# One fused two-block forward pass on one core: where the VectorE work of 128 gathered tokens stands in its queue, and which engine writes a fourth of the one-hots

## The chip, the core and the metric

The kernel runs on one core of one Trainium2 chip. Its time is in device microseconds (us), the median of its runs. The profile names the engines PE (TensorE: matmul, and PEld for its weight loads), DVE (VectorE), ACT (ScalarE), POOL (GpSimd) and SP (SyncE, which only issues DMAs here); a trailing q is the engine's queue. [...]

## What is computed

The reference runs two blocks of two layers each on 256 tokens of 1024 channels. The first block is a mixer (an mLSTM, a block attention and a compressed attention side by side) and a feed-forward of 4096 channels. The second block works on the 256 tokens and, in its first layer, on 256 context tokens too: attention, and then a layer of experts picked by product keys:

```python
v1, i1 = lax.top_k(s1, 16)
v2, i2 = lax.top_k(s2, 16)
top_s, pos = lax.top_k(cand_s, 16)
expert = jnp.take_along_axis(cand_i, pos, axis=-1)
g = jax.nn.softmax(top_s, axis=-1)
act = jax.nn.gelu(jnp.einsum('nhkd,nd->nhk', u_tab[expert], hb))
w = g * act
out = jnp.einsum('nhk,nhkd->nd', w, v_tab[expert])
```

There are 16384 experts with one row of 1024 numbers in each table. A token has 8 heads with 16 experts each, so 128 chosen experts. All is in float32.

## The kernel before

**Split products.** A matmul in this kernel multiplies operands that are cut in two: `split` (line 207) has ACT round the operand to the matmul's format (line 209) and DVE subtract that from the operand (line 210). `mac` (lines 243 to 245) then issues three matmuls, high by high, high by low and low by high. Weights come through `load` (line 118) in tiles of 512 KB on SP's queue, and the two halves lie in the ring `ws`, four buffers, so two weight tiles at a time.

**The order of the work.** Instructions are traced in program order by Python generators. The tile framework then orders each engine's queue by its own plan: an instruction whose inputs the plan holds ready may go ahead of ones that were traced earlier. [...]

**The side generator.** Work on the context tokens is a generator, `aside` (line 1314): context attention, key scores, choice of experts, `spread` for one half of the context tokens, and last `gather` for the other half. The main program moves it on by so many steps at a time: `breathe` (line 92) and `beside` (line 98) in block one and in the second block's first attention, `ahead` (line 1129) by `GP[0]` steps for each expert tile, and the function `side` in `block2` (line 1346) by `GP[1]` steps for each expert tile. The rates stand at the top: `WM`, `WF` (block one), `FN` (line 38: four steps in the norm, and then so many for each yield of `qkv`, `attention` and `attn_out`) and `GP` (line 43).

**Dense experts and the spread.** For 384 rows (the 256 tokens and 128 of the context tokens) the expert layer is computed densely, 128 tiles of 128 experts. `ahead` runs `hidden` (line 1117) for each tile: load 512 KB of the u table, split it, 24 matmuls with 384 columns, gelu on ACT (line 1126), and store of 192 KB to `kept` in DRAM. This is the first hidden pass, about 1332 to 2062 us. `experts` (line 1146) then loads `kept` back, multiplies it by the gate weights G (line 1165), splits it and 512 KB of the v table, and sums in PSUM with 18 matmuls of 512 columns a tile. G comes in loads of 1536 KB for every 8 tiles. While it runs, `side` also moves `ada_rest` on by a step for each odd tile up to the 95th: a load of 512 KB (`in_ada_w`) and one or two DVE instructions (line 777). This is the first sum over experts, about 2062 to 2610 us. The second layer does the same for the 256 tokens (2837 to the end), with no side generator.

G is built by `spread` (line 1061): for every 4 tokens `ones` (line 1067) writes a stationary tile of four one-hots of 128 by 128 in f16, one instruction each on POOL (line 1071), and DVE writes the moving side with three instructions of 512 columns (line 1075). Eight matmuls of 128 columns follow (line 1089). All of it lies in one buffer of the ring `wb` (three buffers), which the loads of the tables also use later. `spread` runs five times with 32 batches: once for the context tokens (about 913 to 1023 us, beside the feed-forward of block one), twice in each hidden pass.

**The gathered tokens.** The other 128 context tokens are computed from their own 128 experts each, by `gather` (line 1275). A slot is the c-th expert of all 128 tokens. For each table there are 128 slots, so 256 in all. `fetch` (line 1282) issues two indirect DMAs on POOL (line 1286) for a pair of slots, 512 KB each, into one buffer of the ring `b8` (three buffers, one of which holds the activations and the sum). Of the first table each slot is a dot product on DVE (line 1304), of the second a weighted addition on DVE (line 1308, 1306 for the first). One step of the generator is one slot. A pair is fetched while the pair before it is computed.

Of the kernel before, what the change touches and what calls it, by code (L numbers as in the profile page):

```python
# [10 lines left out]
F32 = mybir.dt.float32  # L11
# [4 lines left out]
ALU = mybir.AluOpType  # L16
AX = mybir.AxisListType

P = 128
S = 256  # L20
D = 1024
# [13 lines left out]

WM = ({3: 1, 5: 2, 12: 3, 22: 1, 34: 1}, {12: 2, 14: 2, 18: 2, 22: 2, 26: 2, 32: 2, 34: 2, 37: 2})
WF = ((0, 2.0), (0, 3.5))
FN = (4, 2.0, 2.0, 2.0)

P0 = ((0, 1.0), (22, 1.0), (30, 0.8), (72, 0.8))  # L40
P1 = ((2, 1.0), (28, 0.8), (30, 0.72), (79, 0.8))

GP = (0.85, 0.6)

EAR = (1, 1)

# [11 lines left out]
class Net:  # L58
# [148 lines left out]
    def split(self, hi, lo, src):  # L207

        self.nc.scalar.copy(hi, src)  # L209
        self.nc.vector.tensor_sub(lo, src, hi.bitcast(F32))  # L210

    def cut_in_two(self, shape, raw):

# [847 lines left out]
    def spread(self, r, Gd, nb, pm="C", home="k8"):  # L1061


        nc = self.nc
        st, (r, r0) = None, r

        def ones(n):
            E = self.t("wb", [P, 4, 512], F16)
            first = E[:, 0].rearrange("p (j e) -> p j e", e=P)
            for j in range(4):  # L1070
                nc.gpsimd.tensor_scalar(first[:, j], self.iota16, r0[:, n + j:n + j + 1], None, ALU.is_equal)  # L1071
            pairs = [E[:, 1 + i].rearrange("p (h e j) -> p h e j", h=2, j=2) for i in range(3)]
            for i in range(3):
                col = r[:, i, n:n + 4].rearrange("p (h j) -> p h j", j=2)[:, :, None].to_broadcast([P, 2, P, 2])
                nc.vector.tensor_tensor(pairs[i], pairs[0] if i else self.iota2[:, None].to_broadcast([P, 2, P, 2]), col,
                                        op=ALU.mult if i else ALU.is_equal)
            return first, pairs

        E = ones(0)
        yield  # L1080
        for n in range(0, P, 4):
            q, m = divmod(n, NT)
            nxt = ones(n + 4) if n + 4 < P else None
            if m == 0:
                st = self.t(home, [P, P, NT])
            pG = self.p(pm, [P, 4, P])
            for j in range(4):
                for i in range(2):
                    nc.tensor.matmul(pG[:, j], E[0][:, j], E[1][1 + i][:, j // 2, :, j % 2], start=i == 0, stop=i == 1)  # L1089
            nc.scalar.activation(st[:, :, m:m + 4], pG.rearrange("p n e -> p e n"), AF.Copy, scale=1 / GSCALE)  # L1090
            if m == NT - 4:
                nc.sync.dma_start(Gd[:, nb + q], st)
            E = nxt
            yield
# [103 lines left out]
    @staticmethod  # L1198
    def col(mod, s, j):
        return mod[:, s, 8 * j:8 * j + 8]  # L1200
# [74 lines left out]
    def gather(self, idx, g, out):  # L1275


        nc, io = self.nc, self.io
        tables = io["u_rows"], io["v"][0].rearrange("a b d -> (a b) d")
        work = [(t, c) for t in tables for c in range(0, P, 2)]  # L1280

        def fetch(i):
            t, c = work[i]
            r = self.t("b8", [P, 2, D])
            for j in range(2):
                nc.gpsimd.indirect_dma_start(out=r[:, j], out_offset=None, in_=t,
                                             in_offset=bass.IndirectOffsetOnAxis(ap=idx[:, c + j:c + j + 1], axis=0))
            return r

        hr = self.t("b8", [P, 2, D])  # L1290
        nc.sync.dma_start(hr[:, 0], self.hrd)
        h, acc = hr[:, 0], hr[:, 1]
        act = self.t("act", [P, P], bufs=1)
        r = fetch(0)
        for i, (t, c) in enumerate(work):
            if i == P // 2:
                nc.scalar.activation(act, act, AF.Gelu_apprx_tanh)
                nc.vector.tensor_mul(act, act, g)
            nxt = fetch(i + 1) if i + 1 < len(work) else None
            for j in range(2):  # L1300
                a = act[:, c + j:c + j + 1]
                if i < P // 2:
                    junk = self.t("b2", [P, D], mybir.dt.bfloat16)
                    nc.vector.scalar_tensor_tensor(junk, r[:, j], 1.0, h, ALU.mult, ALU.mult, accum_out=a)
                elif i == P // 2 and j == 0:
                    nc.vector.tensor_scalar(acc, r[:, j], a, None, ALU.mult)
                else:
                    nc.vector.scalar_tensor_tensor(acc, r[:, j], a, acc, ALU.mult, ALU.add)  # L1308
                yield
            r = nxt  # L1310
        nc.sync.dma_start(out, acc)
        yield
# [14 lines left out]
    def block2(self, x):  # L1327
# [3 lines left out]

        hT = self.norm_T(fg, x, col(mod, 0, 1), col(mod, 0, 0), between=lambda: self.breathe(FN[0]))
        qT, kT, v = self.beside(self.qkv(fg, 0, hT, True), FN[1])
        oT = self.beside(self.attention(fg, qT, [(kTc, vc), (kT, v)]), FN[2])
        self.beside(self.attn_out(fg, 0, oT, col(mod, 0, 2), x), FN[3])
        hx = self.norm_T(fg, x, col(mod, 0, 4), col(mod, 0, 3), lambda k: (h[0][:, k, 0:S], h[1][:, k, 0:S]))
        hd = lambda k: (h[0][:, k], h[1][:, k])
        far = self.side
        plan = self.routing(0, [hx], Gd[0], ((0, 0), (1, 8)), EAR[0], P0)
        self.ahead(0, hd, ND, self.kept, 128, plan + [(0, far, GP[0], False), (100, self.ada_rest(MID, 48), 0.3, True)])  # L1340
        gates = self.t("k8", [P, 4, 512])
# [4 lines left out]
        def side(e):  # L1346
            if e % 2:
                next(rest, None)
            due[0] += GP[1]
            while due[0] >= 1:  # L1350
# [158 lines left out]
```

## Time and profile before

| | |
|---|---|
| median of 3 runs | 3632.98 us (3625.54 to 3647.02) |
| the profiled execution's own time | 3624.63 us |
| its span, first to last instruction | 3622.9 us |
| PE busy | 3248.7 us, 90% of the span |
| DVE busy | 2513.4 us, 69% |
| ACT busy | 1449.4 us, 40% |
| POOL busy | 978.2 us, 27% |
| moved by DMA | 803.17 MB, mean 222 GB/s |
| mean granted clock of TensorE | 0.953 |

A row of a stretch gives its start and end, its length, then the busy time of each engine with its number of instructions, then the granted clock, the mean busy share of the 16 DMA engines and the rate. A row of waits gives who waited for whom, with the total, the number of times and the longest one. Rows by source line give the number of instructions, their least, median and greatest duration in ns, and the start of the first and the last. A row of the timeline gives start, duration, engine and line, and in brackets the idle time before it with what ended that.

### The profile page before, as it was taken

The numbers are of one execution on the slowest core, as the hardware profiler recorded it, in microseconds if no ns is written. First come the engines' busy times: TensorE is split into PE (matmuls) and PEld (weight loads), VectorE is DVE, ScalarE is ACT, GpSimd is POOL, SyncE is SP. The second block draws the span as 40 slices with busy tenths as digits, with TensorE's granted clock in tenths as the row PEclk, the third lists the DMA queues.
The fourth block names the chain that finished last, engine by engine and source line by source line (L and its number), as shares of the span: only waits on it lengthen the run. The fifth ranks groups of instructions, "written<-read, shape, count | busy, mean of one in ns | idle before, by whom it ended". The sixth has DMA issues, their size and how long they took to land. (4 is left out here: it accounts for less than half of the span.)

```text
span 3622.9 us, 51227 instructions
## 1 busy us (share of the span) xinstructions
PE 3248.7 (90%) x18333; PEld 2772.2 (77%) x18333; DVE 2513.4 (69%) x5177; ACT 1449.4 (40%) x2465; POOL 978.2 (27%) x968
## 2 busy tenths in 40 slices
PE   8999899889756698887779899999989999999999
PEld 6676688768644597887779887777868999988777
DVE  6667556789667897887665576655577888656665
ACT  6543245633323342232223433333344555454443
POOL 0000000000954434787776000000010067830000
PEclk9999999979978899998889999999999999999999
DMA  7456454325467778887886788877523677688885
GB/s 241 151 180 204 151 164 146 108 89 172 159 223 245 253 267 300 291 290 266 287 274 228 254 283 276 266 251 251 178 66 101 198 243 264 241 281 291 288 258 188
DMA packets 340225, 803.17 MB, mean 222 GB/s; under 512 B 31105, under 2 KB 179585, under 8 KB 334593
## 3 DMA queue, kind: packets, MB, share of 16 engines
q1 hardware_dynamic: 303104, 665.66, 56.0%
q0 software_dynamic: 36864, 134.23, 10.8%
q8 instruction: 144, 2.36, 0.3%
q14 instruction: 113, 0.92, 0.1%
HBM read 713.00 MB, written 86.77 MB: 221 GB/s over the span
## 5 line engine op out<-in xcount | busy, mean ns | idle before, releaser
L209 ACT CAST ws<-w 128x1024 fp32r<-128x1024 f32 (+1 forms) x528 | 547.3, 1037 | 1048.8 <-PE psA L244 727.6
L210 DVE TENSOR_TENSOR ws<-w,ws 128x1024 fp32r<-128x1024 f32 (+1 forms) x528 | 640.7, 1215 | 255.3 <-ACT ws L209 253.5
L245 PE MATMUL psA<-b,ws 128*128 128x384 f32 (+1 forms) x2048 | 659.0, 322 | 105.2 <-DVE ws L210 104.3
L1071 POOL TENSOR_SCALAR wb<-iota,R 128x128 f16<-128x128 f16 x640 | 600.3, 954 | 382.3 <-ACT R L1054 279.1
L243 PE MATMUL psA<-b,ws 128*128 128x384 f32 (+1 forms) x2048 | 663.4, 324 | 3.6 <-ACT ws L209 3.6
L244 PE MATMUL psA<-b,ws 128*128 128x384 f32 (+1 forms) x2048 | 652.1, 318 | 0.0
L245 PEld LDWEIGHTS psA<-b,ws 128*128 128x128 f32 x2048 | 398.9, 195 | 119.9 <-DVE ws L210 118.7
L209 ACT CAST k<-wb 128x1024 fp32r<-128x1024 f32 x256 | 269.0, 1051 | 513.3 <-DMA wb<-in_v 513.2
L245 PE MATMUL psC<-k,k 128*128 128x512 f32 x1056 | 422.7, 400 | 25.9 <-DVE k L210 25.2
L243 PE MATMUL psC<-k,k 128*128 128x512 f32 x1056 | 418.6, 397 | 19.6 <-ACT k L209 19.6
L244 PE MATMUL psC<-k,k 128*128 128x512 f32 x1056 | 417.6, 396 | 3.6 <-DVE k L210 3.6
L243 PEld LDWEIGHTS psA<-b,ws 128*128 128x128 f32 x2048 | 399.8, 195 | 4.7 <-ACT ws L209 4.5
L244 PEld LDWEIGHTS psA<-b,ws 128*128 128x128 f32 x2048 | 398.4, 195 | 0.0
L210 DVE TENSOR_TENSOR k<-wb,k 128x1024 fp32r<-128x1024 f32 x256 | 312.4, 1220 | 81.9 <-ACT k L209 81.7
L158 POOL TENSOR_TENSOR rsrf<-rsvf,neghalf 128x1 f32<-128x1 f32 (+5 forms) x38 | 41.9, 1106 | 1206.6 <-DVE rsvf L157 1206.6
L244 PE MATMUL psC<-ws,k 128*128 128x512 f32 (+1 forms) x608 | 250.3, 412 | 25.5 <-DVE ws L210 25.4
L245 PEld LDWEIGHTS psC<-k,k 128*128 128x128 f32 x1056 | 199.2, 189 | 93.2 <-DVE k L210 49.4
L1165 DVE TENSOR_TENSOR k<-k,b 128x384 f32<-128x384 f32 (+1 forms) x256 | 123.7, 489 | 202.7 <-DMA k<-kept 197.8
L243 PE MATMUL psC<-ws,k 128*128 128x512 f32 (+1 forms) x608 | 246.9, 410 | 7.1 <-DVE k L197 4.5
L243 PEld LDWEIGHTS psC<-k,k 128*128 128x128 f32 x1056 | 199.5, 189 | 66.7 <-ACT k L209 23.8
L1308 DVE SCALAR_TENSOR_TENSOR b<-b,act,b 128x1024 f32<-128x1024 f32 x127 | 164.2, 1293 | 120.3 <-DMA b<-in_v,idx 119.7
L245 PE MATMUL psC<-ws,k 128*128 128x512 f32 (+1 forms) x608 | 246.1, 407 | 0.7 <-DVE k L716 0.6
(452 smaller groups left out, 6096.2 us busy)
## 6 DMA issues: line engine op xcount, KB each, us to landing
w<-in_u SPq DMA_DIRECT2D x256, 512.0 KB
wb<-in_v SPq DMA_DIRECT2D x256, 512.0 KB
w<-in_w_ff SPq DMA_DIRECT2D x128, 512.0 KB
wb<-in_ada_w SPq DMA_DIRECT2D x80, 512.0 KB
G<-k SPq DMA_DIRECT2D x32, 1024.0 KB
w<-in_wA SPq DMA_DIRECT2D x48, 512.0 KB
kept<-k SPq DMA_DIRECT2D x128, 192.0 KB
b<-G SPq DMA_DIRECT2D x16, 1536.0 KB
```

Source lines behind the costliest of these rows:

```text
L158: nc.gpsimd.tensor_tensor(r[:m, :cols], v[:m, :cols], self.neghalf[:m, :cols], op=ALU.pow)
L209: self.nc.scalar.copy(hi, src)
L210: self.nc.vector.tensor_sub(lo, src, hi.bitcast(F32))
L243: self.nc.tensor.matmul(out, ah, bh, start=first, stop=False)
L244: self.nc.tensor.matmul(out, ah, bl, start=False, stop=False)
L245: self.nc.tensor.matmul(out, al, bh, start=False, stop=last)
L1071: nc.gpsimd.tensor_scalar(first[:, j], self.iota16, r0[:, n + j:n + j + 1], None, ALU.is_equal)
L1165: nc.vector.tensor_mul(g3, g3, Gs[:, :, j])
L1308: nc.vector.scalar_tensor_tensor(acc, r[:, j], a, acc, ALU.mult, ALU.add)
```

## The change

`split` keeps its DVE subtraction in `self.mark`. Every DVE instruction of `gather` is traced inside `issue_after(self.mark)`: an edge without a semaphore that keeps it behind the subtraction traced last, in DVE's own queue. The rates `FN` and `GP` change. In `ones` the fourth of the four one-hots is written by DVE.

```diff
-FN = (4, 2.0, 2.0, 2.0)
+FN = (4, 1.5, 1.5, 1.5)
...
-GP = (0.85, 0.6)
+GP = (0.8, 0.9)
...
         self.nc.scalar.copy(hi, src)
-        self.nc.vector.tensor_sub(lo, src, hi.bitcast(F32))
+        self.mark = self.nc.vector.tensor_sub(lo, src, hi.bitcast(F32)).ins
...
             for j in range(4):
-                nc.gpsimd.tensor_scalar(first[:, j], self.iota16, r0[:, n + j:n + j + 1], None, ALU.is_equal)
+                eng = nc.vector if j == 3 else nc.gpsimd
+                eng.tensor_scalar(first[:, j], self.iota16, r0[:, n + j:n + j + 1], None, ALU.is_equal)
...
             for j in range(2):
                 a = act[:, c + j:c + j + 1]
-                if i < P // 2:
-                    junk = self.t("b2", [P, D], mybir.dt.bfloat16)
-                    nc.vector.scalar_tensor_tensor(junk, r[:, j], 1.0, h, ALU.mult, ALU.mult, accum_out=a)
-                elif i == P // 2 and j == 0:
-                    nc.vector.tensor_scalar(acc, r[:, j], a, None, ALU.mult)
-                else:
-                    nc.vector.scalar_tensor_tensor(acc, r[:, j], a, acc, ALU.mult, ALU.add)
+                with self.tc.issue_after(self.mark):
+                    if i < P // 2:
+                        junk = self.t("b2", [P, D], mybir.dt.bfloat16)
+                        nc.vector.scalar_tensor_tensor(junk, r[:, j], 1.0, h, ALU.mult, ALU.mult, accum_out=a)
+                    elif i == P // 2 and j == 0:
+                        nc.vector.tensor_scalar(acc, r[:, j], a, None, ALU.mult)
+                    else:
+                        nc.vector.scalar_tensor_tensor(acc, r[:, j], a, acc, ALU.mult, ALU.add)
                 yield
```

## Rows read from the trace of the kernel before

**Rows 1.** The page, part 1: busy us of each engine, share of the span, instructions.

```profile
PE 3248.7 (90%) x18333; PEld 2772.2 (77%) x18333; DVE 2513.4 (69%) x5177; ACT 1449.4 (40%) x2465; POOL 978.2 (27%) x968
```

**Rows 2.** Stretches from 1332 on: us, busy us of each engine, PEclk, DMA share, GB/s.

```profile
1332.00:1450.00 118.00, 100.78 (x519) 97.91 (x518) 96.05 (x241) 34.12 (x49) 47.21 (x36) 0.93 0.84 290
...
1650.00:1900.00 250.00, 191.60 (x1058) 181.58 (x1059) 167.30 (x205) 63.48 (x99) 194.99 (x174) 0.87 0.82 279
...
1900.00:2000.00 100.00, 99.73 (x651) 96.75 (x650) 54.55 (x86) 38.51 (x59) 58.39 (x56) 1.00 0.69 228
```

**Rows 3.** PE's waits, 1332 to 2062: us in total, times, longest.

```profile
PE psA L245 <- DVE ws L210: 103.7, 38, 7.2
```

**Rows 4.** VectorE's timeline from 1816 to 1846: start, us, what, idle before.

```profile
1822.91 1.28 DVE L1308 SCALAR_TENSOR_TENSOR b<-b,act,b 128x1024 f32<-128x1024 f32 x1 [5.07 <-DMA b<-in_v,idx]
...
1824.12 1.22 DVE L210 TENSOR_TENSOR ws<-w,ws 128x1024 fp32r<-128x1024 f32 x1
```

**Rows 5.** Line 1126, once for each hidden expert: 1332 to 1450, 1650 to 1900, 1900 to 2000.

```profile
L1126 ACT ACTIVATE k<-psA x22: 478/485/493, 1332.2 to 1446.5; 128x384 f32<-128x384 f32 x22
...
L1126 ACT ACTIVATE k<-psA x35: 482/484/490, 1659.4 to 1899.4; 128x384 f32<-128x384 f32 x35
...
L1126 ACT ACTIVATE k<-psA x21: 477/486/490, 1903.7 to 1996.8; 128x384 f32<-128x384 f32 x21
```

**Rows 6.** The slots' instructions: line 1304 in 1020 to 1233 and 1233 to 1332, then all of line 1308.

```profile
L1304 DVE SCALAR_TENSOR_TENSOR b<-b,b x71: 1209/1219/1284, 1030.0 to 1231.9; 128x1024 bf16<-128x1024 f32 x71
...
L1304 DVE SCALAR_TENSOR_TENSOR b<-b,b x28: 1209/1222/1237, 1231.9 to 1325.0; 128x1024 bf16<-128x1024 f32 x28
...
L1308 DVE SCALAR_TENSOR_TENSOR b<-b,act,b x127: 1257/1285/1446, 1431.9 to 1888.5; 128x1024 f32<-128x1024 f32 x127
```

**Rows 7.** Waits over the whole span around the slots: us in total, times, longest.

```profile
POOL b L1286 <- DVE b L1304: 143.0, 40, 15.2
...
DVE b L1308 <- DMA b<-in_v,idx: 119.7, 61, 6.0
```

**Rows 8.** Stretches of the second block's two layers, attention and then key scores of each.

```profile
1057.00:1233.00 176.00, 117.85 (x438) 87.36 (x438) 140.31 (x292) 57.16 (x137) 82.26 (x70) 0.80 0.70 237
...
1233.00:1332.00 99.00, 80.55 (x547) 74.72 (x548) 89.98 (x240) 36.53 (x68) 35.75 (x30) 0.88 0.79 268
...
2640.00:2767.00 127.00, 116.22 (x546) 92.65 (x546) 94.55 (x257) 67.41 (x179) 8.92 (x11) 0.97 0.26 84
...
2767.00:2837.00 70.00, 65.73 (x513) 63.48 (x514) 49.59 (x169) 33.15 (x62) 0.56 (x1) 0.95 0.39 123
```

**Rows 9.** GpSimd's one-hots: line 1071 over the span, and PE's wait for them up to 1020.

```profile
L1071 POOL TENSOR_SCALAR wb<-iota,R x640: 592/702/4086, 913.4 to 3209.8; 128x128 f16<-128x128 f16 x160
...
PE psB L1089 <- POOL wb L1071: 20.4, 42, 1.5
```

**Rows 10.** VectorE, lines 1057 and 1075: duration ns least, median, most.

```profile
L1057 DVE CAST R<-k x4: 220/220/220, 1464.8 to 3086.0; 128x128 f16<-128x128 f32 x4
...
L1075 DVE TENSOR_TENSOR wb<-iota,R x160: 398/426/642, 914.4 to 3206.8; 128x512 f16<-128x512 f16 x160
```

**Rows 11.** Stretches of the first sum over experts, and of the second hidden pass.

```profile
2062.00:2500.00 438.00, 409.59 (x1735) 322.28 (x1734) 284.40 (x426) 146.89 (x203) 0.00 (x0) 0.99 0.84 270
...
2500.00:2610.00 110.00, 110.00 (x477) 89.17 (x476) 60.63 (x85) 40.63 (x55) 0.00 (x0) 1.00 0.67 209
...
2900.00:3200.00 300.00, 298.35 (x2684) 294.88 (x2683) 226.84 (x483) 154.93 (x253) 226.90 (x247) 0.99 0.74 252
```

**Rows 12.** Line 1165, once for each summed expert: 2062 to 2500, and 2500 to 2620.

```profile
L1165 DVE TENSOR_TENSOR k<-k,b x101: 549/554/560, 2071.4 to 2498.2; 128x384 f32<-128x384 f32 x101
...
L1165 DVE TENSOR_TENSOR k<-k,b x27: 551/559/560, 2501.7 to 2605.7; 128x384 f32<-128x384 f32 x27
```

**Rows 13.** Two stretches inside the first hidden pass, 50 and 10 us long.

```profile
1550.00:1600.00 50.00, 46.18 (x298) 43.67 (x297) 44.16 (x100) 21.26 (x31) 45.01 (x44) 1.00 0.88 308
...
1560.00:1570.00 10.00, 10.00 (x74) 9.69 (x72) 6.01 (x12) 4.33 (x7) 9.00 (x11) 1.00 1.01 392
```

## The prediction

> **What bounds the kernel now.** I read the page first, then busy time by stretch, then the waits and VectorE's timeline of the poorest stretch. PE is busy 90% of the span [rows 1], so what can be won is PE's idle time and the time at the lower clock. [...] PE's idle time in this pass has one cause: 103.7 us in 38 waits, up to 7.2 us each, of a line 245 matmul for the low half from VectorE's line 210 [rows 3]. VectorE isn't too slow there, it stands: a slot's instruction waited 5.07 us for its gathered rows, and the subtraction that PE needed ran right behind it [rows 4]. Over the span the second half of the slots held VectorE idle for 119.7 us [rows 7].
>
> The slots also run ahead of their place in the program. Counting yields, 200 steps are asked for in block one, and 189 come before the first slot, so 11 slots are traced by then. FN gives 4 + 30 × 2.0 = 64 more in the attention, GP 0.85 × 128 = 109 in the hidden pass, and the last 72 come at 0.6 a tile, up to tile 120 of the sum. On the chip 71 were done by 1233 (traced: 75), 28 more by 1332, and the last started at 1888.5 [rows 6], in the hidden pass. So 256 − 99 = 157 ran there, not 109: the plan had moved them forward, ahead of subtractions that PE was about to need.
>
> **The change, step by step.** Everything is summed against the profiled execution.
>
> *A. The order in the hidden pass.* With the edge, a slot can't pass the subtraction of the tile at which it is traced. Its place becomes 0.8 a tile: 102 slots instead of 157. A pair's fetch is issued when the pair before the last has been used, and its first slot is then due three slots later, 3 × 4.85 / 0.8 = 18 us, against 119.7 us / 61 = 2 us by which it was late on average [rows 7]. So the wait should go. What is late next is PE itself. Today's rates are 118 / 22 = 5.36 us a tile with slots and no spread, 250 / 35 = 7.14 at worst, and 100 / 21 = 4.76 with spread and no slots [rows 2, 5]. I take 4.85, near the last, the rest for slots that still stand badly: 128 × 4.85 = 621 us against the 730 from 1332 to 2062, **−109**. The bounds are 4.76 (−121) and 5.36 (−44). VectorE can carry this: it is busy 54.55 us in those 100 [rows 2], and 21 × 0.8 slots of 1.285 us [rows 6] add 22.
>
> *B. Attention and key scores.* FN now gives 4 + 30 × 1.5 = 49 slots instead of 64, and the 28 that ran from 1233 to 1332 can't run there any more, since nothing is traced between the attention and the hidden pass. The second layer's like stretches, which have no slots, take 127 and 70 us, where these take 176 and 99 [rows 8]. So the key scores win up to 29; the attention paid 49 us for some 59 slots (71 less the dozen before 1057), 0.83 each, and with 10 fewer wins 8. Sum **−37**; from −10 (the layers differ: the second projects the context too) to −54 (the edge also ends waits in the attention).
>
> *C. A fourth of the one-hots.* Line 1071 ran 640 times, median 702 ns [rows 9]; 160 of these leave POOL. Only in block one does PE wait for them, 20.4 us [rows 9]; a batch that is a quarter shorter should end about half of that: **−12**, between 0 and −20. On VectorE the price of a 128x128 f16 compare is not in the trace. It lies between the 0.22 us of a cast of that size and the 0.43 of a compare four times as wide [rows 10]; it is nearest to the cast, so 160 × 0.22 = 35 us. It waits for the same `wb` buffer as line 1075, and the splits queue behind it. Of this 7 us fall in block one, 14 in each hidden pass, beside PE's work; in the second one PE is busy 298.35 of 300 us, VectorE 226.84 [rows 11]. I cost it at **0**, at most +14 if that cover is gone in the second pass.
>
> [...] Line 1071 takes from 592 to 4086 ns for one and the same shape [rows 9], so POOL is held up by something. [...]
>
> *D. The sum over experts.* 256 − 11 − 49 − 102 = 94 slots now fall here, at 0.9 a tile, up to tile 105. POOL is free for their fetches (0.00 us busy from 2062 to 2500 [rows 11]), SP's queue isn't passed, and VectorE goes from 284.40 / 101 = 2.82 us a tile to 2.82 + 0.9 × 1.285 = 3.97, below the 438 / 101 = 4.34 that a tile takes [rows 6, 11, 12]. But the loads run at 270 GB/s here, with the engines 0.84 busy [rows 11]. A tile moves 0.524 MB of v, 0.197 of `kept`, 0.197 of G and 0.262 of `in_ada_w`: 1.18 MB, which at 4.34 us is 272 GB/s, as the row says. With 0.9 × 0.524 MB more it is 1.65; after the 95th tile 1.39. The first 105 tiles thus move 96 × 1.65 + 9 × 1.39 = 171 MB. The best 50 us beside slots had 308 GB/s, the best 10 us 392 [rows 13]. At 306 this takes 559 us, and 23 tiles at 110 / 27 = 4.07 follow, 94: 653 against 548, **+104**. Bounds: +180 at today's 270, +0 at 392, where DMA no longer sets the time.
>
> [...]
>
> Sum: −109 − 37 − 12 + 104 = **−54** on 3624.63, that is 3571; the runs' median is 8 above the profiled execution, so **3579** is the forecast. All bounds at once reach from 3624.63 − 195 to 3624.63 + 140.
>
> **Rivals.**
> 1. *The DMA engines still have room.* For: 392 GB/s over 10 us, and at present the sum's loads wait for free buffers as well as for the engines (0.84 busy). Against: no 50 us above 308. Between 340 GB/s (+49) and 392 (0), say +25: sum −133, 3633 − 133 = 3500.
> 2. *Slower: the sum over experts keeps today's rate.* Three `wb` buffers carry v and `in_ada_w`, and each load takes longer beside a fetch, so its buffer comes free later and the rate doesn't rise above 270. That is +180: sum +22, 3655. It decides below 280 GB/s, where 171 MB take 611 us and eat the other three terms (−158). For: 0.84 busy now. Against: the hidden pass moves 279 to 290 beside slots [rows 2].
> 3. *The edges bind nothing.* If the plan already had each slot behind its subtraction, only C would be left: −12, 3621. Against: 157 slots ran where 109 are traced.
> [...]
>
> **Chances.** Forecast 0.47, rival 1 0.23, rival 2 0.17, rival 3 0.06, rival 4 0.07. A measurement of this kernel can tell about 0.5%, 18 us, from no change. Faster: 0.43 of the forecast and rival 1, 0.66. Same: 0.04 of the forecast, 0.03 of rival 2, rival 3, and 0.03 of rival 4, 0.16. Slower: the rest of rivals 2 and 4, 0.18. The forecast's own range, with A, B and D each off by half of what their bounds allow, is about 3535 to 3625. The range for 8 in 10 reaches to rival 1 and past rival 2: 3490 to 3670.
>
> **What would show it.** A: from 1332 on 4.7 to 5.0 us a tile (line 1126), PE's wait for line 210 below 30 us instead of 103.7, the granted clock at 0.97 or more, and line 1308 running into the sum over experts, about 94 slots of it. B: the key scores near 70 us. C: line 1071 480 times, PE's wait for it about 10 us, and a new row of f16 compares on VectorE near 0.22 us. D: the first sum over experts near 650 us at 300 GB/s or more, and slots that hardly wait. The prediction is wrong if PE still waits for line 210 in the hidden pass, if the sum over experts stays near 560 us, or if it grows past 700.

## The result and the profile after

The changed kernel takes **3488.64 us** in the median of 3 runs (3481.16 to 3489.97) against 3632.98: a ratio of 0.9591 [0.9541, 0.9642]. That is −144 us, where the forecast was −54. The direction was right; the size was not, and the time lies just under the lower end of the range, 3490.

The page's part 1 of the kernel after (busy us, share, instructions), which answers to [rows 1]:

```profile
PE 3209.4 (92%) x18333; PEld 2744.0 (79%) x18333; DVE 2536.7 (73%) x5337; ACT 1451.1 (42%) x2465; POOL 873.0 (25%) x808
```

VectorE has 160 instructions more, POOL 160 fewer. PE's busy time fell by 39 us with the same instructions, and the mean granted clock of the span, a share of full speed, rose from 0.953 to 0.963: fewer of them ran at the lower clock (0.50 from 1815 to 1820 us in the trace of before, where matmuls of 384 columns start 0.32 us apart, against 0.18 at 1.00).

The table cuts each profiled execution of this study into five stages, and a sixth part for what is left. Its borders are the starts of lines and one end: the last addition of block one's feed-forward, the last addition of the second block's first attention, the first gelu, the end of the last gelu (128 tiles), and the last multiplication by G. Slots are those that start in the hidden pass and in the sum over experts.

| kernel | block one | attention | key scores | hidden pass (slots) | sum over experts (slots) | rest | span |
|---|---|---|---|---|---|---|---|
| before | 1056.0 | 198.7 | 77.5 | 730.3 (158) | 543.2 (0) | 1017.2 | 3622.9 |
| after | 1044.9 | 162.2 | 72.0 | 585.9 (101) | 611.2 (94) | 1012.0 | 3488.2 |
| e1_edges | 1056.6 | 191.8 | 71.8 | 587.6 (107) | 603.7 (73) | 1008.0 | 3519.5 |
| e2_rates | 1057.3 | 162.5 | 75.7 | 757.2 (175) | 546.0 (0) | 1018.5 | 3617.2 |
| e3_onehots | 1042.2 | 195.2 | 77.0 | 720.4 (158) | 547.6 (0) | 1017.0 | 3599.4 |
| e4_edges_rates | 1062.6 | 163.8 | 72.4 | 583.8 (101) | 611.5 (94) | 1018.0 | 3512.1 |
| e5_half_rows | 1035.9 | 166.0 | 72.2 | 582.6 (101) | 573.0 (94) | 1011.5 | 3441.2 |
| e6_half_vector | 1039.2 | 165.3 | 71.5 | 586.0 (101) | 635.2 (94) | 1015.3 | 3512.5 |
| e7_more_hidden | 1034.6 | 167.9 | 71.6 | 586.1 (126) | 608.9 (68) | 1016.2 | 3485.3 |
| e8_fewer_hidden | 1040.5 | 164.8 | 71.3 | 587.6 (76) | 627.1 (119) | 1017.1 | 3508.4 |
| e9_as_many | 1041.4 | 167.2 | 72.1 | 605.2 (151) | 566.9 (43) | 1017.3 | 3470.1 |
| e10_ada_apart | 1043.7 | 164.7 | 71.4 | 586.1 (101) | 611.8 (94) | 1014.0 | 3491.7 |
| e11_ada_apart_gp | 1040.7 | 169.4 | 71.3 | 590.9 (126) | 583.9 (68) | 1016.1 | 3472.3 |
| e12_ada_apart_before | 1055.8 | 197.8 | 76.8 | 727.9 (158) | 523.1 (0) | 1015.6 | 3597.0 |
| e13_as_many_apart | 1043.6 | 164.2 | 71.6 | 602.2 (151) | 561.0 (43) | 1014.6 | 3457.2 |
| e14_all_hidden | 1033.8 | 166.4 | 72.0 | 668.9 (189) | 520.1 (4) | 1014.3 | 3475.5 |
| e15_half_rows_gp | 1046.0 | 165.0 | 72.0 | 579.8 (126) | 571.5 (68) | 1016.9 | 3451.2 |

From before to after: block one −11, attention −36, key scores −6, **hidden pass −144**, **sum over experts +68**, rest −5: −135 between the two spans.

Busy time by stretch (columns as in [rows 2]): the whole hidden pass and the sum before, then the hidden pass, the sum, and the sum's part with slots after.

```profile
1332.00:2062.00 730.00, 622.11 (x3563) 597.92 (x3561) 502.82 (x897) 228.28 (x338) 456.51 (x410) 0.93 0.80 273
2062.00:2606.00 544.00, 515.59 (x2193) 408.23 (x2192) 341.10 (x505) 186.25 (x256) 0.00 (x0) 0.99 0.81 259
```

```profile
1279.00:1865.00 586.00, 577.00 (x3563) 564.18 (x3561) 445.65 (x942) 228.77 (x340) 334.01 (x294) 0.99 0.84 289
1865.00:2476.00 611.00, 542.64 (x2199) 421.92 (x2200) 450.95 (x598) 188.48 (x255) 124.86 (x90) 0.96 0.91 311
1865.00:2400.00 535.00, 466.64 (x1871) 360.24 (x1872) 410.83 (x543) 159.16 (x217) 124.86 (x90) 0.95 0.94 325
```

In the hidden pass PE is now busy 577.00 of 586 us at a clock of 0.99: little is left to win there but PE's own work. Of the 144 us, 99 were PE's idle time (108 us before, 9 after) and 45 its busy time (622.11 against 577.00), with the clock up from 0.93 to 0.99. In the sum it is the other way round: while slots run, the DMA engines are 0.94 busy and PE stands 68 of 535 us. Of the 68 us that the whole sum grew by, some 40 are PE's idle time and 27 its busy time (542.64 against 515.59), with the clock down from 0.99 to 0.96.

PE's waits after, in the hidden pass (us in total, times, longest), against the 103.7 us of [rows 3]:

```profile
PE psA L245 <- DVE ws L210: 4.8, 5, 2.7
PE psA L243 <- ACT ws L209: 3.7, 1, 3.7
```

VectorE's timeline after, inside that pass, shows the new order beside [rows 4], for a slot of the first table and one of the second:

```profile
1563.51 1.31 DVE L210 TENSOR_TENSOR ws<-w,ws 128x1024 fp32r<-128x1024 f32 x1
1564.74 1.21 DVE L1306 SCALAR_TENSOR_TENSOR b<-b,b 128x1024 bf16<-128x1024 f32 x1
...
1716.11 1.23 DVE L210 TENSOR_TENSOR ws<-w,ws 128x1024 fp32r<-128x1024 f32 x1 [1.43 <-ACT ws L209]
1717.26 1.28 DVE L1310 SCALAR_TENSOR_TENSOR b<-b,act,b 128x1024 f32<-128x1024 f32 x1
```

Now the subtraction runs first and the slot right behind it, without a wait. Before, the slot stood 5.07 us and the subtraction came after it. That sample is typical: in the trace of before, 30 of the 38 waits of [rows 3], 96 of their 103.7 us, were for a subtraction that had a slot waiting for its rows at most four instructions and 10 us ahead of it on VectorE.

Of the slots' instructions and the one-hots after, by line (as [rows 6] and [rows 9], line 1304 being 1306 now, 1308 being 1310, 1071 being 1072; line 1310 in the stretch of the sum alone):

```profile
L1306 DVE SCALAR_TENSOR_TENSOR b<-b,b x128: 1195/1217/1390, 1017.5 to 1647.5; 128x1024 bf16<-128x1024 f32 x128
...
L1310 DVE SCALAR_TENSOR_TENSOR b<-b,act,b x94: 1271/1279/1315, 1875.9 to 2398.4; 128x1024 f32<-128x1024 f32 x94
...
L1072 POOL TENSOR_SCALAR wb<-iota,R x480: 591/864/4911, 921.3 to 3075.6; 128x128 f16<-128x128 f16 x160
...
L1072 DVE TENSOR_SCALAR wb<-iota,R x160: 235/271/564, 922.4 to 3073.1; 128x128 f16<-128x128 f16 x160
```

94 slots run in the sum, up to 2398. And the waits around the slots over the whole span, as in [rows 7]:

```profile
POOL b L1287 <- DVE b L1310: 437.9, 54, 18.1
...
DVE b L1306 <- DMA b<-in_u_rows,idx: 32.6, 20, 7.7
```

The wait has changed sides. The second half's slots no longer wait for their rows (119.7 us before); POOL waits for the slots instead, 437.9 us. Of these 373.4 fall in the sum, where POOL has nothing else to do; in the hidden pass PE's weight loads waited 1.4 us in all for POOL's one-hots.

### The profile page after: what moved, and what is told of

Same layout as the page of the kernel before. It is cut to its first block, busy times and chain, and to the rows that moved or that the text cites. A ratio compares the mean times of both kernels' runs of the same rounds, so it can differ in the third digit from the quotient of the medians.

```text
span 3488.2 us, 51167 instructions
## 1 busy us (share of the span) xinstructions
PE 3209.4 (92%) x18333; PEld 2744.0 (79%) x18333; DVE 2536.7 (73%) x5337; ACT 1451.1 (42%) x2465; POOL 873.0 (25%) x808
## 5 line engine op out<-in xcount | busy, mean ns | idle before, releaser
L243 PE MATMUL psA<-b,ws 128*128 128x384 f32 (+1 forms) x2048 | 647.6, 316 | 3.7 <-ACT ws L209 3.7
L245 PE MATMUL psA<-b,ws 128*128 128x384 f32 (+1 forms) x2048 | 638.8, 312 | 5.6 <-DVE ws L210 5.2
L244 PE MATMUL psA<-b,ws 128*128 128x384 f32 (+1 forms) x2048 | 637.3, 311 | 0.0
L1072 POOL TENSOR_SCALAR wb<-iota,R 128x128 f16<-128x128 f16 x480 | 495.1, 1045 | 420.8 <-ACT R L1054 287.0
L243 PE MATMUL psC<-k,k 128*128 128x512 f32 x1056 | 427.9, 405 | 50.2 <-ACT k L209 50.0
L245 PE MATMUL psC<-k,k 128*128 128x512 f32 x1056 | 427.5, 406 | 26.8 <-DVE k L210 26.3
L244 PE MATMUL psC<-k,k 128*128 128x512 f32 x1056 | 425.5, 403 | 9.2 <-DVE k L210 9.2
L245 PEld LDWEIGHTS psA<-b,ws 128*128 128x128 f32 x2048 | 385.6, 188 | 9.7 <-DVE ws L210 9.7
L243 PEld LDWEIGHTS psA<-b,ws 128*128 128x128 f32 x2048 | 387.3, 189 | 4.2 <-ACT ws L209 4.0
L244 PEld LDWEIGHTS psA<-b,ws 128*128 128x128 f32 x2048 | 386.0, 188 | 0.0
L1287 POOL DMA_INDIRECT b<-in_v,idx x128 | 171.1, 1337 | 481.4 <-DVE b L1310 437.9
L243 PEld LDWEIGHTS psC<-k,k 128*128 128x128 f32 x1056 | 203.5, 193 | 105.8 <-ACT k L209 62.1
L245 PEld LDWEIGHTS psC<-k,k 128*128 128x128 f32 x1056 | 203.4, 193 | 92.8 <-DVE k L210 47.1
L244 PE MATMUL psC<-ws,k 128*128 128x512 f32 (+1 forms) x608 | 246.3, 405 | 16.5 <-DVE ws L210 16.3
L243 PE MATMUL psC<-ws,k 128*128 128x512 f32 (+1 forms) x608 | 243.6, 405 | 7.4 <-ACT k L209 5.9
L244 PEld LDWEIGHTS psC<-k,k 128*128 128x128 f32 x1056 | 204.0, 193 | 57.8 <-DVE k L210 12.4
L245 PE MATMUL psC<-ws,k 128*128 128x512 f32 (+1 forms) x608 | 243.4, 402 | 0.7 <-DVE amxb L892 0.6
L1287 POOL DMA_INDIRECT b<-in_u_rows,idx x128 | 150.6, 1177 | 302.5 <-DVE b L1306 215.9
```

Source lines behind the costliest of these rows:

```text
L243: self.nc.tensor.matmul(out, ah, bh, start=first, stop=False)
L244: self.nc.tensor.matmul(out, ah, bl, start=False, stop=False)
L245: self.nc.tensor.matmul(out, al, bh, start=False, stop=last)
L1072: eng.tensor_scalar(first[:, j], self.iota16, r0[:, n + j:n + j + 1], None, ALU.is_equal)
```

## The experiments

**One part of the change at a time.** Four kernels: the edges alone, the rates alone, the one-hots alone, and edges with rates.

`e1_edges` is the kernel before with the mark and the edge, at the old rates:

```diff
-        self.nc.vector.tensor_sub(lo, src, hi.bitcast(F32))
+        self.mark = self.nc.vector.tensor_sub(lo, src, hi.bitcast(F32)).ins
...
+                with self.tc.issue_after(self.mark):
```

> The kernel before with the edges alone: slots behind the split traced last, FN (4, 2.0, 2.0, 2.0) and GP (0.85, 0.6) as before, all one-hots on POOL. If the order in VectorE's queue is what cost the time: in the first hidden pass PE's wait for line 210 falls from 103.7 us to under 20, 128 tiles at about 4.6 us make 590 us instead of 730 (-140), 72 slots move into the sum over experts (+45), the attention wins about 10: near 3525 us. If instead it was the number of slots in the hidden pass and in the attention, the edges alone leave most of the waits: 3600 us or more.

3528.04 us, 0.9725 [0.97, 0.975]. Its stretches of the hidden pass and of the sum, and PE's wait in the former:

```profile
1320.00:1908.00 588.00, 575.22 (x3564) 562.76 (x3563) 445.23 (x869) 229.12 (x340) 395.99 (x362) 0.99 0.85 293
1908.00:2512.00 604.00, 543.67 (x2210) 429.38 (x2211) 426.51 (x579) 186.31 (x255) 95.78 (x70) 0.94 0.88 297
```

```profile
PE psA L245 <- DVE ws L210: 10.8, 6, 5.2
```

The edges alone bring the whole gain of the hidden pass (588 us, clock 0.99, the wait from 103.7 to 10.8 us) and nearly the whole loss of the sum (+60 of +68), with 73 slots there. Key scores win 6 us, the attention 7.

`e2_rates` is the kernel before with the new rates alone:

```diff
-FN = (4, 2.0, 2.0, 2.0)
+FN = (4, 1.5, 1.5, 1.5)
-GP = (0.85, 0.6)
+GP = (0.8, 0.9)
```

> The kernel before with FN (4, 1.5, 1.5, 1.5) and GP (0.8, 0.9) alone, no edges, all one-hots on POOL. If the order counts: the plan still moves slots forward past the subtractions, more than 102 of them run in the hidden pass and PE waits there for line 210 by 80 us or more; 3600 to 3650 us. If the number counts: the slots fall where they are traced, near 3500 us.

3628.29 us, 0.9994 [0.9976, 1.0012]. The attention wins its 36 us (162.5), and the hidden pass gives 27 of them back (757.2), since the slots taken from the attention run there, still ahead of subtractions. PE's wait in the hidden pass:

```profile
PE psA L245 <- DVE ws L210: 123.5, 47, 8.4
```

So the attention's gain belongs to `FN`, and without the edges it is worth nothing. The raised `GP[1]` does nothing by itself: no slot is left for the sum.

`e3_onehots` is the kernel before with the fourth one-hot on VectorE:

```diff
-                nc.gpsimd.tensor_scalar(first[:, j], self.iota16, r0[:, n + j:n + j + 1], None, ALU.is_equal)
+                eng = nc.vector if j == 3 else nc.gpsimd
+                eng.tensor_scalar(first[:, j], self.iota16, r0[:, n + j:n + j + 1], None, ALU.is_equal)
```

> The kernel before with the fourth one-hot on VectorE alone. Expected: 10 to 15 us less before the second block's attention (PE waited 20.4 us for POOL there), nothing elsewhere: 3618 to 3630 us. [...]

3589.18 us, 0.9873 [0.9838, 0.9907], some 44 us of the shared 3632.92 where 10 to 15 were expected. The profiled execution shows 24 of them: block one −14, hidden pass −10; the rest is not explained. PE's wait for POOL's one-hots up to 1040:

```profile
PE psB L1090 <- POOL wb L1072: 11.8, 14, 3.9
```

That is about half of the 20.4 us of [rows 9]. `e4_edges_rates` takes this part out of the kernel after (the same diff, reversed).

> The changed kernel with all four one-hots on POOL again. If the one-hots pay only in block one: 8 to 15 us slower than the changed kernel, near 3500 us, with the same hidden pass (585 us) and the same sum over experts (612 us). If POOL's fetches wait behind its one-hots in the hidden pass, the waits for line 210 come back and it is 30 us slower or more. If the one-hots on VectorE hold POOL up, it is faster than the changed kernel.

3510.98 us, 0.9672 [0.9645, 0.97]. The hidden pass is the same without the moved one-hots (583.8 against 585.9), block one is 18 us longer, and the wait in it is back:

```profile
PE psB L1089 <- POOL wb L1071: 21.0, 37, 1.6
```

Over all profiles, the 12 with the moved one-hots end block one at 1033.8 to 1046.0, the 5 without at 1055.8 to 1062.6: means of 1040.5 and 1057.7, so the part is worth 17 us there.

**Is it the order, or the smaller number of slots in the hidden pass?** Both fell at once. `e9_as_many` is the kernel after with a rate at which 151 slots run there, nearly the 158 of before:

```diff
-GP = (0.8, 0.9)
+GP = (1.2, 0.5)
```

> The changed kernel with GP = (1.2, 0.5): about 154 slots in the hidden pass, as many as the kernel before ran there (157), but behind their subtractions; 42 in the sum over experts. If the order alone made the kernel before slow there: the hidden pass stays within 25 us of 586 (before: 730), PE waits there for line 210 less than 25 us, and the total is 3460 to 3500. If the number of slots or their bytes (334 GB/s would be needed) made it slow: 640 us or more for the hidden pass, and the total above 3520.

3470.13 us, 0.9558 [0.9542, 0.9574]. Its hidden pass, and PE's wait in it:

```profile
1281.00:1886.00 605.00, 581.16 (x3561) 565.46 (x3559) 501.67 (x991) 228.47 (x339) 415.25 (x342) 0.99 0.91 323
```

```profile
PE psA L245 <- DVE ws L210: 15.5, 15, 3.0
```

605 us instead of 730 with 96% of the slots: of the 144 us, 125 come with the edges at nearly the same number of slots, and 19 with the smaller number (the moved one-hots, which this kernel has too, change nothing in this pass once the edges are there, by `e4_edges_rates`). The edges do two things, though: they put a slot behind its subtraction, and they spread the slots. Before, the 158 stood in the first 91 tiles, 1.7 a tile at 6.1 us each, and the last 37 tiles took 4.7; here they come at 1.2 a tile throughout. `e14_all_hidden`, below, has 1.5 a tile behind their subtractions and takes 5.2 us a tile. So the spreading has a share in the 125 us, which no run separates. `e7_more_hidden` and `e8_fewer_hidden` stand on either side of the kernel after, with `GP` at (1.0, 0.65) and (0.6, 1.15):

> The changed kernel with GP = (1.0, 0.65): 128 slots in the hidden pass instead of 102, 68 in the sum over experts instead of 94. If the hidden pass is bound by PE with room on VectorE and in the DMA: it stays at 585 to 595 us, and the sum over experts, 26 x 0.524 MB = 14 MB lighter at 325 GB/s, wins up to 40: about 3455. If the hidden pass is full: PE's waits for line 210 come back there and the total is 3490 or more.

> The changed kernel with GP = (0.6, 1.15): 77 slots in the hidden pass, 119 in the sum over experts. If the hidden pass is bound by PE already: no gain there (580 to 586 us), and the sum over experts pays 25 x 0.524 MB = 13 MB at 325 GB/s, 40 us: about 3530. If slots still cost time in the hidden pass, it gains 20 us or more there.

3501.47 us, 0.9653 [0.9637, 0.9669] and 3508.81, 0.9668 [0.9636, 0.97]. With 76, 101 and 126 slots the hidden pass takes 587.6, 585.9 and 586.1 us: slots in it are free up to about one a tile, near what the first branch of both expectations has. The sum takes 627.1, 611.2 and 608.9 with 119, 94 and 68: the first 25 slots taken out are worth 16 us, the next 26 only 2, where up to 40 were expected of either step. The profiled execution of `e7_more_hidden` is 14 us below the median of its runs, so its stages say less than its ratio.

**What makes the sum longer?** Three suspects: the bytes of the slots, their time on VectorE, or the ring `wb` that v and `in_ada_w` share. `e5_half_rows` fetches half rows of the second table, with as many VectorE elements:

```diff
+        half = io["v"][0].rearrange("a b (h d) -> (a b h) d", h=2)
...
+                    nc.gpsimd.indirect_dma_start(out=r[:, j, 0:D // 2], out_offset=None, in_=half,
...
-                        nc.vector.scalar_tensor_tensor(acc, r[:, j], a, acc, ALU.mult, ALU.add)
+                        nc.vector.scalar_tensor_tensor(acc.rearrange("p (i d) -> p i d", i=2), r[:, j, None, 0:D // 2].to_broadcast([P, 2, D // 2]), a, acc.rearrange("p (i d) -> p i d", i=2), ALU.mult, ALU.add)
```

> The changed kernel, where a slot of the second table gathers rows of 2 KB instead of 4 KB, from other places, and VectorE reads each half row twice, so that its instructions keep their length; it leaves out half of the second table's rows. 94 slots in the sum over experts then move 25 MB less. If the bytes set the time there (325 GB/s): that pass falls from 612 us by 50 to 65, to about 550 to 560, and the total to about 3430. If VectorE's queue sets it: 612 us and 3489 stay.

3440.70 us, 0.9481 [0.9465, 0.9497]. The sum falls from 611 to 573, short of the 550 to 560 expected by bytes and far from the 612 of the other branch; so of the 68 us that 94 slots cost, 38 go with half of the bytes. `e6_half_vector` fetches whole rows and computes on half of them:

```diff
-                        nc.vector.scalar_tensor_tensor(acc, r[:, j], a, acc, ALU.mult, ALU.add)
+                        nc.vector.scalar_tensor_tensor(acc[:, 0:D // 2], r[:, j, 0:D // 2], a, acc[:, 0:D // 2], ALU.mult, ALU.add)
```

> The changed kernel, where VectorE adds up only the first 512 channels of each slot of the second table; the fetches stay whole. It leaves out the other half of that sum. In the sum over experts VectorE is spared 94 x 0.65 = 61 us. If the bytes set the time there: within 10 us of the changed kernel, 3480 to 3495. If VectorE's queue sets it: 30 to 60 us less, about 3440.

3514.5 us, 0.9689 [0.9672, 0.9705]: slower than the kernel after, though a slot in the sum took 0.75 us of VectorE instead of 1.28. The sum grew to 635, which neither branch had. So sparing VectorE won nothing. In the sum PE's wait for line 210 is 60.6 us here, 19.3 after:

```profile
DVE k L1166 <- DMA k<-kept: 102.8, 42, 8.6
DVE b L777 <- DMA wb<-in_ada_w: 84.8, 29, 9.4
PE psC L245 <- DVE k L210: 60.6, 32, 6.5
```

The first two rows are 51.9 and 23.5 us after, and 50 of the 60.6 us were for subtractions that had one of these two instructions, waiting for its load, at most four instructions and 10 us ahead of them on VectorE. It is the same kind of wait as in the hidden pass before, with instructions that have no edge. Why they stand ahead more often here is open; that another duration lets the plan order the queues anew is a guess.

For the ring, `e10_ada_apart` loads the 48 `in_ada_w` tiles of the sum into another ring:

```diff
-            w = self.load("wb", [P, D], io["ada_w"][i - EARLY])
+            w = self.load("wb" if i < 48 else "k8", [P, D], io["ada_w"][i - EARLY])
```

`e11_ada_apart_gp` has that with `GP` (1.0, 0.65), and `e12_ada_apart_before` has it in the kernel before.

> The changed kernel, where the 48 loads of in_ada_w that stand beside the sum over experts go into a buffer of the ring k8 instead of wb; same bytes, same instructions. The three wb buffers then serve the v loads alone. If the sum over experts waits because a slot delays the instruction that frees a wb buffer: its 611 us fall by 30 to 60, to 550 to 580, and the total to 3430 to 3460. If the bytes set the time (325 GB/s): 611 us stay within 10, 3480 to 3495.

> As the one before, with GP = (1.0, 0.65) too: 68 slots in the sum over experts instead of 94. By freed buffers: 545 to 570 us for that pass, total 3420 to 3450, the fastest of all. By bytes: as e7_more_hidden, 609 us and 3501.

> The kernel before, with the same 48 loads in k8. Its sum over experts has no slots: 543 us, 15 of them above the 128 x 4.12 that PE needs. By freed buffers: 530 to 540 us there and a total of 3615 to 3628. By bytes: no change.

3485.9 us, 0.9596 [0.958, 0.9612]; 3473.77, 0.9556 [0.9529, 0.9584]; 3602.2, 0.9931 [0.9907, 0.9955]. With 94 slots the other ring changes nothing (611.8 against 611.2 us), with 68 it saves 25 (583.9 against 608.9), with none 20 (523.1 against 543.2). ACT's waits for the loads of v go the same way: with no slots from 334.3 to 125.6 us, with 68 from 360.4 to 170.6, with 94 only from 352.7 to 263.2. The reading that fits is that the two limits take turns: the ring holds the loads back while the DMA engines have room (0.81 busy over the sum with no slots), and at 94 slots they have little (0.91). The test isn't clean, since `k8` also holds the split halves of v, and ACT's splits now wait for line 777. But these waits are 64.6 us with 94 slots and 131.5 and 155.7 with 68 and none, where the move pays, so they don't explain why it wins nothing at 94. The expectations of `e11_ada_apart_gp` were missed by 14 us in the sum and 24 in total, those of `e12_ada_apart_before` passed by 7 and 13. The sums of `e10_ada_apart` and `e11_ada_apart_gp`:

```profile
1865.00:2477.00 612.00, 542.35 (x2199) 427.75 (x2198) 451.44 (x602) 187.79 (x256) 130.74 (x90) 0.93 0.90 312
```

```profile
1872.00:2456.00 584.00, 528.46 (x2181) 416.04 (x2182) 420.92 (x576) 184.36 (x253) 87.81 (x64) 0.96 0.88 303
```

`e15_half_rows_gp` is `e5_half_rows` with `GP` (1.0, 0.65), so with the ring shared and fewer bytes:

> The changed kernel with GP = (1.0, 0.65) and rows of 2 KB for the slots of the second table, read twice each (half of the second table's rows left out): 68 slots in the sum over experts. If the bytes set its 609 us: 68 x 0.262 = 18 MB less, 550 to 565 us. If the buffers do: 590 us or more.

3453.58 us, 0.9525 [0.9494, 0.9556]. Its sum takes 571.5 us with 68 half slots (550 to 565 were expected by bytes, 590 or more by buffers), `e5_half_rows` 573.0 with 94: here the number of slots doesn't matter. Against 608.9 with 68 whole rows, half of the bytes are again worth 37 us, in a stage whose engines are on average no busier than 0.87. So the bytes cost time below the engines' limit too, as fits loads that take longer to free a shared buffer; that step is argued, not shown.

**Both limits together.** `e13_as_many_apart` has the other ring and `GP` (1.2, 0.5); `e14_all_hidden` the other ring and (1.5, 0.5), which leaves 4 slots for the sum.

> The changed kernel with GP = (1.2, 0.5) and the 48 loads of in_ada_w in k8: 43 slots in the sum over experts. If buffers still count where the engines aren't full: the sum over experts 540 to 555 us instead of 567, total 3445 to 3460. If not: 3470.

> The changed kernel with GP = (1.5, 0.5) and the 48 loads in k8: about 190 slots in the hidden pass, next to none in the sum over experts. If only the order counted, the hidden pass would stay near 605 us and the total fall to about 3430. By bytes: 190 x 0.524 + 128 x 0.721 + 21 MB are 213 MB, at 325 to 340 GB/s 625 to 655 us; the sum over experts is back at 523 to 535; total 3450 to 3480.

3455.63 us, **0.952 [0.9485, 0.9554]**, and 3489.02, 0.9621 [0.9588, 0.9655]. The first beats the kernel before clearly and the kernel after by 33 us in the medians, 26 by the ratios, where the two intervals overlap by 0.0013; that of `e10_ada_apart`, which differs from it by the rates alone, lies apart. Hidden pass 602.2, sum 561.0: the total came as expected for buffers that still count, the sum not (540 to 555), and against `e9_as_many` it is only 6 us shorter, so that question stays open. The second has the shortest sum, 520.1, and pays for it in the hidden pass, more than by the bytes that the expectation counted (625 to 655 us):

```profile
1272.00:1941.00 669.00, 603.51 (x3563) 580.18 (x3561) 544.74 (x1026) 226.15 (x338) 453.32 (x382) 0.95 0.90 321
```

```profile
PE psA L245 <- DVE ws L210: 60.6, 34, 6.8
```

```profile
DVE b L1310 <- DMA b<-in_v,idx: 81.6, 39, 6.4
```

At 189 slots (1.5 a tile) they wait for their rows again, and what stands behind them on VectorE waits with them: about half of the 60.6 us (29.5) were for subtractions with such a slot ahead. The edge orders; only a rate that leaves fetches their time takes the wait away.

## Why the prediction was wrong in size

**A, the order in the hidden pass: mechanism right, term too small, and its bound wrong.** Forecast 621 us (−109, at best −121), measured 585.9 (−144). 102 slots were forecast there and 101 ran; the wait was to be below 30 us and is 4.8; the clock 0.97 or more and is 0.99. What failed is the best case: "I take 4.85, near the last". 4.76 us a tile [rows 5] was no floor, since that stretch held more spread than its share. Its matmuls of line 1089, beside those of the whole hidden pass after (busy us, mean ns | idle before):

```profile
L1089 PE MATMUL psC<-wb 128*128 128x128 f16 x136 | 10.8, 220 | 0.0
```

```profile
L1090 PE MATMUL psC<-wb 128*128 128x128 f16 x512 | 40.6, 220 | 0.0
```

136 of them are 17 batches in 21 tiles; the pass has 64 in 128. From the rows of before, PE's time without spread is (99.73 − 10.8) / 21 = 4.23 us a tile, and 64 × 10.8 / 17 / 128 = 0.32 for spread makes 4.55: 583 us. The 21 is low, too: the 651 matmuls less 136 are 515, at 24 a tile 21.5 tiles, which makes 4.14 + 0.32 = 4.46 and 571 us. Measured are 577.00 us of PE and 9 of waits. The stretch without waits gave the answer; I read its time for each tile and not what was in it. The 0.09 us added for "slots that still stand badly" weren't needed either. That makes 35 of the 90 us missed.

**B, attention and key scores: right in sum by luck, wrong in its parts.** Forecast −37, measured −42. But −29 was for the key scores and −8 for the attention, and it came out as −6 and −36. The border at 1233 [rows 8] was 22 us too early: the attention's last addition is at 1254.7. And `e2_rates` shows 36 us of attention won by the rates alone, so the slots that left it (77 before, 60 after) cost some 2 us each and not the 0.83 that I spread over all of them. The key scores' 70 us came (72.0), but by the right border they took only 77.5 before.

**C, the one-hots: right in block one, too small in all.** Forecast −12, measured in block one −11 in this pair and −17 over all profiles; the wait fell from 20.4 to 11.7 us. The price on VectorE was taken as 0.22 us and is 0.271 in the median, inside the bounds; the cover held, with the rest of the program at −5. Whole runs show more than the bound of 20: 44 us alone (`e3_onehots`), of which its stages don't place some 20, and 22 between the medians of `e4_edges_rates` and the kernel after.

**D, the sum over experts: mechanism right, term too large.** Forecast +104 (653 us at 306 GB/s), measured +68 (611). 94 slots ran there as forecast, and none of them waited for its rows. "At 306 this takes 559 us" is the step that failed: the part with slots ran at 325 GB/s, 0.94 of the engines, for 535 us. 171 MB at 325 are 526 us, and with the 94 of the tail 620. The best 50 us of the trace of before was a sample of what was asked for, not of what could be had (nor was it the best: 1560 to 1610 had 315 GB/s). The tail was shorter as well, 76 us for 20 tiles. That makes 36 us more. The others are B and C (5 − 1), the rest of the program (5), and the difference between the medians, −144, and the spans, −135 (10, unrounded): 35 + 36 + 4 + 5 + 10 = 90.

**The rivals.** Rival 1 (3500) is nearest in time: DMA had room, if less than it assumed (340 or more). No run shows the 340, and so the +25, for so long a stretch: the kernel after ran at 325 GB/s for 535 us, and `e8_fewer_hidden` at 335 for 550 us (the mean of eleven stretches from 1864 to 2414, which have 322 to 354). Rival 2 falls by the same 325: the rate rose to it from 270; yet the ring that it blamed costs time where fewer slots run, as `e11_ada_apart_gp` and `e12_ada_apart_before` show. Rival 3 falls by `e1_edges`. Rival 4, in the chances slower or the same, falls by `e3_onehots` and `e4_edges_rates`: the moved one-hots help in both, by 44 and 22 us in the medians.

## What to carry to other kernels

Where a planner may advance side work in an engine's queue, one edge that keeps it behind the critical instruction can be worth more than a change of rates (here 0.9725 against 0.9994); but a side instruction that waits for a transfer still held up what stood behind it (29.5 of PE's 60.6 us in `e14_all_hidden`), so the rate has to leave the transfer its time. A stretch of the trace without waits gives the floor of a stage only after its mix of work has been set to the stage's own (here 4.76 us a tile as read, 4.46 to 4.55 so set, 4.51 of PE measured). Work that is moved out of one stage is paid for in the next one by what limits that one (here −144 us in the hidden pass, +68 in the sum at 0.94 of the DMA engines): share it out so that neither stage pays alone (the best of the rates tried here were 1.2 slots a tile in one and 0.5 in the other), not to where one of them is free.

## What was not expected of the hardware

- The DMA engines sustained 325 GB/s for 535 us of mixed loads and gathers, and the best 50 us after had 375:

```profile
2160.00:2210.00 50.00, 46.90 (x198) 36.60 (x197) 42.27 (x56) 14.94 (x20) 11.79 (x10) 1.00 1.04 375
```

- VectorE writes a one-hot in 271 ns in the median; POOL's 480 that remain take 864, against 702 for the 640 of before [rows 9]. The traces don't show the moved one-hots as the cause. With the one-hots moved alone (`e3_onehots`) POOL's median falls to 630. By stage they got faster in block one (787 to 631 ns) and in the second hidden pass (702 to 612), and slower only in the first hidden pass, where `e4_edges_rates`, with every one-hot on POOL, is slow as well. In block one that kernel has 599, so the median moves without the change, too. The first hidden pass before, of `e4_edges_rates`, and after:

```profile
L1071 POOL TENSOR_SCALAR wb<-iota,R x256: 592/632/4086, 1465.7 to 1988.0; 128x128 f16<-128x128 f16 x128
L1071 POOL TENSOR_SCALAR wb<-iota,R x256: 590/846/2657, 1404.2 to 1799.0; 128x128 f16<-128x128 f16 x128
L1072 POOL TENSOR_SCALAR wb<-iota,R x192: 591/922/2478, 1384.4 to 1779.8; 128x128 f16<-128x128 f16 x192
```
